# Spreading two softmax weights over 64 feature rows: GpSimd copies and transposes, or loads of DRAM rows

## The chip, the cores and the metric

One core of one Trainium2 chip. The time is the device time of one launch in microseconds; beside it stands one profiled execution, which is somewhat longer than the others. The core has TensorE (matrix products and transposes), VectorE, ScalarE, GpSimd, and a set of DMA engines. DMAs are issued from the queues of SyncE, ScalarE and GpSimd; a queue goes through its instructions in order, so an instruction that waits holds up all that is behind it on its engine.

## What is computed

Two layers of a decoder trunk on 512 tokens of width 1024. Each layer has a mixing part (windowed attention beside retention, joined by gates) and a feed-forward part. The change touches the end of the attention alone. There are three groups of six heads of 64 features: plain windows, windows with keys at every 4th token, and windows with keys at every 16th. The outputs of the groups are added with weights in proportion to their softmax denominators:

```
o   = einsum('bghnqk,bghnke->bghnqe', p / l, vb)
lse = m + log(l)
wts = softmax(stack(lses), axis=0)
y_a = sum(wts[..., None] * stack(outs), axis=0)
```

In the kernel the second and third group are computed under one softmax, in an order of tokens in which every 4th token stands together. So two "orders" are left, 0 (tokens in their own order) and 1 (token 4l + r stands at place l of part r), and each head and token has two weights.

## The kernel before

All large products are split in a high and a low half (`whi`, `wlo`) and take three matmuls each. ScalarE makes the high half by a cast (line 346), VectorE the low one by a subtraction (line 354). TensorE runs these products one after the other, and other work is threaded between them: a list of small steps (`side`), from which a step is taken each time that some matmuls have been written down. The program is written in that order. A planner then orders each engine's instructions by this order and by when it expects their inputs to be ready, so a small instruction can stand earlier on its engine than in the text.

The attention of a layer goes over three pairs of heads. For a pair, `attention_pair` makes two lists. `ops` holds, for each of four tiles of 128 tokens, the scores (line 517, with exponentials at line 535), their transposes and copies (lines 545 and 546) and the products with the values (line 558; copy to `y` at line 559), and at the end `swap`, which stores maxima and sums of order 1 to DRAM (line 573). `tail` holds what comes after: `swapped` loads them back in the order of the tokens (line 576), `weigh` computes the two weights on 128 token partitions (lines 582 to 593) and stores those of order 1 to DRAM (line 592), `weighed` loads these back in the other order (line 598). Then, for each order, `expand` copies each weight 64 times along the free dimension on GpSimd (line 605), `turn_weights` transposes the four tiles on TensorE into PSUM (line 611), so that features stand on partitions and tokens along the row as in `y`, and `combine` multiplies on VectorE and adds (lines 616 to 620).

The tail of pairs 0 and 1 is put between the steps of the next pair, at fixed places (line 959). That of pair 2 runs beside the rotary products, the value and gate products and the first retention scores (lines 965 and 1045). A tiny copy from `latest["sT"]`, the last transposed score tile (lines 582 and 597), keeps the planner from moving the step ahead of that tile.

Of the kernel before, what the change touches and what calls it, by code (L numbers as in the profile page):

```python
# [12 lines left out]
F32 = mybir.dt.float32  # L13
# [3 lines left out]
ALU = mybir.AluOpType  # L17
# [3 lines left out]
P = 128  # L21
S = 512
D = 1024
KD = D // P
NI = S // P
DEPTH = 2
HD = 64
HPG = 6
NG = 3
# [27 lines left out]
def hybrid_kernel(ctx, tc, x, x_t, w_first, rel_t, b_cols, b_rows, w_in, w_attn_proj, w_ret_proj, w_out,  # L57
# [3 lines left out]
    pe, act, dve, pool = nc.tensor, nc.scalar, nc.vector, nc.gpsimd  # L61
# [4 lines left out]
    sm = ctx.enter_context(tc.tile_pool(name="sm", bufs=4, side="right"))  # L66
    rawp = ctx.enter_context(tc.tile_pool(name="rawp", bufs=8, side="right"))
    drp = ctx.enter_context(tc.tile_pool(name="drp", bufs=1, space=DRAM))
# [34 lines left out]
    def psum(name="px"):  # L103
        return psm.tile([P, S], F32, tag="mm", name=name)
# [11 lines left out]
    def work(name):  # L116
        return wk.tile([P, S], F32, tag="w2", name=name)
# [387 lines left out]

    latest = {}

    def attention_pair(hp, qk, v, yp, bias, yaT):


        y = yp()
# [46 lines left out]
                        mm(px[cs, od * P:(od + 1) * P], vs[j][:, cs], sTs[od][:, hh, j * P:(j + 1) * P], j == j1, j == 1)  # L558
            act.copy(out=y[:, :, i], in_=px[:, :2 * P].rearrange("p (o t) -> p o t", o=2))

        fa = sm.tile([P, 2, NI, 2], F32, tag="fa", name="fa", bufs=2)
        mb = sm.tile([P, NI, 4], F32, tag="mb", name="mb", bufs=2)
        wb = sm.tile([P, NI, 2], F32, tag="wb", name="wb", bufs=2)

        exd = drp.tile([S, 4], F32, tag="exd", name="exd", bufs=2)
        exd2 = drp.tile([S, 2], F32, tag="exd2", name="exd2", bufs=2)

        def swap():

# [8 lines left out]
        def weigh():  # L578
            mn = sm.tile([P, NI, 2], F32, tag="mn", name="mn", bufs=2)
            ea = sm.tile([P, 2, NI, 2], F32, tag="ea", name="ea", bufs=2)  # L580
            wa = sm.tile([P, NI, 2], F32, tag="wa", name="wa", bufs=2)
            dve.tensor_copy(mn, latest["sT"][:, 0, P:P + 2 * NI].rearrange("p (i h) -> p i h", i=NI))
            dve.tensor_tensor(out=mn, in0=nm[:, 0], in1=mb[:, :, 0:2], op=ALU.min)
            dve.tensor_tensor(out=ea[:, 0], in0=mn, in1=nm[:, 0], op=ALU.subtract)
            dve.tensor_tensor(out=ea[:, 1], in0=mn, in1=mb[:, :, 0:2], op=ALU.subtract)
            act.activation(out=ea, in_=ea, func=AF.Exp)
            dve.tensor_tensor(out=wa, in0=ea[:, 0], in1=ls[:, 0], op=ALU.mult)
            dve.tensor_tensor(out=wb, in0=ea[:, 1], in1=mb[:, :, 2:4], op=ALU.mult)
            dve.tensor_tensor(out=wa, in0=wa, in1=wb, op=ALU.add)
            dve.reciprocal(out=wa, in_=wa)  # L590
            dve.tensor_tensor(out=wb, in0=ea[:, 1], in1=wa, op=ALU.mult)
            act.dma_start(exd2.rearrange("(i p) c -> p i c", p=P), wb)
            dve.tensor_tensor(out=fa[:, 0], in0=ea[:, 0], in1=wa, op=ALU.mult)

        def weighed():

            act.copy(out=fa[:, 1], in_=latest["sT"][:, 0, P:P + 2 * NI].rearrange("p (i h) -> p i h", i=NI))
            act.dma_start(fa[:, 1], exd2.rearrange("(l r) c -> l r c", r=4))

        wide_, weights = {}, {}  # L600

        def expand(od):

            wide_[od] = work("fe")
            pool.tensor_copy(out=wide_[od].rearrange("p (i h e) -> p i h e", i=NI, h=2),
                             in_=fa[:, od].unsqueeze(3).to_broadcast([P, NI, 2, HD]))

        def turn_weights(od):
            px = weights[od] = psum()
            for i in range(NI):  # L610
                pe.transpose(px[:, i * P:(i + 1) * P], wide_[od][:, i * P:(i + 1) * P], ident)  # L611

        def combine(od):
            yo = y[:, od].rearrange("p i t -> p (i t)")
            if od == 0:
                dve.tensor_tensor(out=yaT[:, hp], in0=yo, in1=weights[od], op=ALU.mult)
            else:
                dve.tensor_tensor(out=yo, in0=yo, in1=weights[od], op=ALU.mult)
                yr = yaT[:, hp].rearrange("p (l r) -> p r l", r=4)
                dve.tensor_tensor(out=yr, in0=yr, in1=y[:, od], op=ALU.add)  # L620

# [3 lines left out]
                places[(0, 7, 14, 20)[i] + at].append(lambda f=f, i=i: f(i))  # L625
        ops = [f for p_ in places for f in p_ or [nothing]]
        ops.append(swap)
        steps = [[lambda f=f, od=od: f(od) for f in (expand, turn_weights, combine)] for od in range(2)]
        tail = [swapped, weigh] + steps[0] + [weighed] + steps[1]
        return ops, tail  # L630

    VB = 288
# [10 lines left out]
    def layer(ly, cp):  # L643
# [12 lines left out]
        csp = yap  # L656
        cos = csp.tile([P, S], F32, name="cos")
        sin = csp.tile([P, S], F32, name="sin")

        def slot(name="op", dt=F32R):  # L660
            return opp.tile([P, 2, S], dt, tag="op", name=name)
# [62 lines left out]
        with stage("attn") as ap_, stage("attw", 4) as aw:  # L724
# [212 lines left out]
            for hp in range(HPG // 2):  # L937
                if hp:
                    for g in range(2):
                        qk_slot(hp, g)  # L940
                if hp == 2:
                    qk_put(2, 2, 1, wstat(us, 1))
                if hp:
                    qk_group((hp, 0), (hp, 1))
                if hp == 1:
                    us = qk_units(2, 2)
                    qk_slot(2, 2)
                    qk_put(2, 2, 0, wstat(us, 0))
                drain()
                ops, t_ = attention_pair(hp, [qk[hp, g] for g in range(NG)], load_v(hp), outputs_last if hp == HPG // 2 - 1 else outputs_, bias, yaT)  # L950
                if hp + 1 < HPG // 2:
                    ops.insert(17, lambda hp=hp: load_bias(hp + 1))
                if hp == 0:
                    if ly == 0:
                        for tab in (cos, sin):
                            pool.tensor_copy(out=tab[:, :1], in_=qk[0, 0][:, 0, :1])
                    pool.dma_start(cos, c_cos)
                    pool.dma_start(sin, c_sin)
                for at, f in zip((31, 30, 28, 22, 20, 18, 13, 12, 3), reversed(tail)):
                    ops.insert(at, f)  # L960
                side.extend([nothing] * (3, 3, 8)[hp] + ops)
                tail = t_
                pace(25 if hp < 2 else 32)
            n = [nothing]
            side.extend(n * 3 + tail[:1] + n * 8 + tail[1:3] + n * 2 + tail[3:4] + n * 2 + tail[4:5] + n + tail[5:6])
            pace(42)
            rotary(0)
            vg = ret_values_gates(0)
# [4 lines left out]
        with ret:  # L973
# [59 lines left out]
            for h in range(RH):  # L1033
                if h:
                    side.extend(ops)
                    pace(18)
                    rotary(h)
                    drain()
                    vg = ret_values_gates(h)
                    side.extend(turns)  # L1040
                ops = ret_scores(h)
                if h:
                    side.extend([nothing] + ops)
                else:
                    side.extend([nothing] + ops + tail[6:7] + [nothing] * 2 + tail[7:8] + [nothing] + tail[8:] + [nothing])
                pace(15 if h == 0 else 32)
                run(vg)
                drain()
                ops, turns = ret_outputs(h)
# [554 lines left out]
```

## Time and profile before

| | us |
|---|---|
| median of 3 runs | 2082.54 (2082.49 to 2083.14) |
| the profiled execution | 2089.8 |
| its span | 2088.0 |
| TensorE busy in the span | 2069.8 |
| VectorE / ScalarE / GpSimd busy | 1644.6 / 1146.5 / 252.2 |

TensorE's clock was granted at 0.998. Lines of the profile name an engine (PE is TensorE, PEld its weight load, DVE is VectorE, ACT ScalarE, POOL GpSimd), a line of the kernel, and the tiles written and read; a q behind the engine means its queue, where DMAs are issued. The DRAM tile `exd2` shows as `exd` in these rows, since trailing digits are left out, and the wide tile of weights as `fe`. Matmuls overlap, so the time that one takes from TensorE is read from the starts of neighbours, not from its duration.

### The profile page before, as it was taken

The page shows a single profiled execution, that of the slowest core. Times are in us where ns is not written, and L with a number is a line of the kernel's source. Part 1 is how long each engine was busy: PE and PEld are TensorE (multiplying, and loading weights), DVE is VectorE, ACT ScalarE, POOL GpSimd, SP SyncE. Part 2 cuts the span into 40 slices and gives each one's busy share as a digit, 9 for nine tenths or more (in the row PEclk, how much of TensorE's full clock was granted, in tenths as well). Part 3 has the DMA queues.
Part 4 walks back from the last instruction along what each step waited for, and adds up shares of the span by engine and source line. Part 5 has one row for each costly group of instructions (what it writes and reads, how often), then busy time and mean ns, then how long its engine had stood idle before and what let it go on. Part 6 is the DMA issues. An engine that isn't in the chain of part 4 may idle for free.

```text
span 2088.0 us, 33561 instructions
## 1 busy us (share of the span) xinstructions
PE 2069.8 (99%) x13090; PEld 1851.0 (89%) x13090; DVE 1644.6 (79%) x2335; ACT 1146.5 (55%) x1746; POOL 252.2 (12%) x236
## 2 busy tenths in 40 slices
PE   9999999999999999999999999999999999999998
PEld 9989888888788898999899898888888889989897
DVE  7757888786797698887777578797868877988876
ACT  6576655565654364555355766455655534655551
POOL 1001111100021101011020011111100211110101
PEclk9999999999999999999999999999999999999999
DMA  7855466766979368868258555667669882786871
GB/s 233 220 139 143 123 169 169 188 165 164 284 158 277 72 159 203 193 162 220 81 167 222 143 134 132 169 160 201 179 154 282 175 264 70 180 206 162 200 192 43
DMA packets 298991, 363.21 MB, mean 174 GB/s; under 512 B 21968, under 2 KB 209488, under 8 KB 298832
## 3 DMA queue, kind: packets, MB, share of 16 engines
q1 hardware_dynamic: 208544, 251.17, 38.0%
q0 software_dynamic: 62592, 97.01, 25.9%
q10 hardware_dynamic: 27696, 12.89, 2.2%
q8 instruction: 102, 1.67, 0.3%
q14 instruction: 57, 0.47, 0.1%
HBM read 339.45 MB, written 21.57 MB: 173 GB/s over the span
## 4 chain that ended last, share of the span: by engine, by line
PE 89%; issue 4%; DMA 3%; DVE 2%; ACT 1%; POOL 0%; ACTq 0%; SPq 0%; POOLq 0%; DVEq 0%
PE ps L96 81%; PE px L96 6%; DMA y_d<-yt 1%; PE px L545 1%; DMA raw<-in_w_in 1%; DVE wlo L354 1%; PE px L1021 1%; ACT whi L346 0%; PE px L208 0%; PE px L1234 0%; POOL ry L150 0%; DMA xc<-in_x_t 0%; ACTq L1024 0%; PE px L611 0%; DMA v_d<-sn 0%
## 5 line engine op out<-in xcount | busy, mean ns | idle before, releaser
L354 DVE TENSOR_TENSOR wlo<-raw,whi 128x1024 fp32r<-128x1024 f32 (+1 forms) x518 | 602.1, 1172 | 192.3 <-ACT whi L346 175.3
L346 ACT CAST whi<-raw 128x1024 fp32r<-128x1024 f32 (+1 forms) x518 | 516.4, 1007 | 387.7 <-PE ps L96 145.3
L96 PE MATMUL ps<-xs,whi 128*128 128x256 f32 x2176 | 399.2, 285 | 0.4 <-ACT sn L773 0.4
L96 PE MATMUL ps<-whi,xs 128*128 128x512 f32 (+1 forms) x1152 | 347.6, 372 | 0.5 <-ACT sn L487 0.5
L96 PEld LDWEIGHTS ps<-xs,whi 128*128 128x128 f32 x2176 | 339.7, 192 | 4.7 <-issue 1.7
L96 PE MATMUL ps<-xh,whi 128*128 128x256 f32 (+1 forms) x1104 | 318.7, 291 | 0.7 <-ACT xh L107 0.7
L96 PE MATMUL ps<-xl,whi 128*128 128x256 f32 (+1 forms) x1104 | 315.8, 287 | 0.1
L96 PE MATMUL ps<-xh,wlo 128*128 128x256 f32 (+1 forms) x1104 | 315.1, 286 | 0.0
L96 PE MATMUL ps<-xs,wlo 128*128 128x256 f32 x1088 | 307.9, 283 | 0.0
L96 PEld LDWEIGHTS ps<-whi,xs 128*128 128x128 f32 x1152 | 210.0, 188 | 34.9 <-ACT sn L487 0.9
L96 PEld LDWEIGHTS ps<-xh,whi 128*128 128x128 f32 x1104 | 211.1, 192 | 7.9 <-issue 1.7
L96 PEld LDWEIGHTS ps<-xl,whi 128*128 128x128 f32 x1104 | 211.7, 192 | 2.9 <-DVE xl L108 0.9
L96 PE MATMUL ps<-wlo,xs 128*128 128x512 f32 (+1 forms) x576 | 213.3, 370 | 0.8 <-DVE wlo L354 0.8
L96 PEld LDWEIGHTS ps<-xh,wlo 128*128 128x128 f32 x1104 | 211.5, 192 | 1.4
L96 PEld LDWEIGHTS ps<-xs,wlo 128*128 128x128 f32 x1088 | 208.7, 192 | 0.0
L96 PE MATMUL ps<-whi,xh 128*128 128x512 f32 (+1 forms) x512 | 194.4, 380 | 4.2 <-ACT whi L346 2.6
L96 PE MATMUL ps<-wlo,xh 128*128 128x512 f32 (+1 forms) x512 | 191.1, 374 | 0.3 <-DVE wlo L354 0.3
L96 PE MATMUL ps<-whi,xl 128*128 128x512 f32 (+1 forms) x512 | 191.1, 374 | 0.0
L337 POOL DMA_DIRECT2D raw<-in_w_in x80 | 96.2, 1209 | 717.8 <-DMA raw<-in_w_in 263.8
L370 DVE TENSOR_TENSOR raw<-raw 128x1024 f32<-128x1024 f32 (+1 forms) x148 | 171.7, 1168 | 0.8
L96 PE MATMUL ps<-whi,ht 128*128 128x512 f32 x544 | 170.2, 391 | 0.0
L107 ACT CAST whi<-raw 128x1024 fp32r<-128x1024 f32 (+1 forms) x100 | 100.0, 1016 | 84.3 <-PE ps L96 68.0
(226 smaller groups left out, 3216.3 us busy)
## 6 DMA issues: line engine op xcount, KB each, us to landing
raw<-in_w_in SPq DMA_DIRECT2D x168, 512.0 KB, 5.2
raw<-in_w_in POOLq DMA_DIRECT2D x64, 512.0 KB, 8.1
raw<-in_w_ffn_up SPq DMA_DIRECT2D x64, 512.0 KB, 4.6
raw<-in_w_ffn_down SPq DMA_DIRECT2D x52, 512.0 KB, 4.6
raw<-in_w_ffn_gate SPq DMA_DIRECT2D x44, 512.0 KB, 5.2
raw<-in_w_ffn_gate POOLq DMA_DIRECT2D x40, 512.0 KB, 6.8
raw<-in_w_in SPq DMA_DIRECT2D x48, 256.0 KB, 4.8
raw<-in_w_ret_proj SPq DMA_DIRECT2D x24, 512.0 KB, 5.8
```

The lines of the kernel that those rows point to most:

```text
L96: pe.matmul(ps, lhsT=a, rhs=b, start=start, stop=stop, skip_group_check=True)
L107: c = act.copy(out=hi, in_=src)
L337: pool.dma_start(r, self.src({"P1": "B12", "P3": "B22"}[n], u), accum_op=ALU.add)
L346: c = act.copy(out=h, in_=src)
L354: dve.tensor_tensor(out=l, in0=src, in1=h.bitcast(F32), op=ALU.subtract)
L370: dve.tensor_tensor(out=r, in0=r, in1=self.t["B22" if n == "P2" else "B21", u], op=ALU.add)
L545: pe.transpose(px[:, hh, j * P:(j + 1) * P], ss[od][:, hh, j * P:(j + 1) * P], ident)
L1021: pe.transpose(px[:, t * P:(t + 1) * P], ys[i][:, t * P:(t + 1) * P], ident)
```

## The change

The weights are no longer spread over the 64 features of a head on chip. `weigh` writes both orders' weights into one small tile and stores it to DRAM as four rows of 512 tokens (two orders, two heads), element by element. `spread` then loads for each order two of these rows, each broadcast into 64 partitions of a tile `fe` of 128 x 512. `combine` multiplies `y` by `fe`; for order 1 it reads `fe` in steps of four instead of having the weights loaded back in the other order. `weighed`, `expand` and `turn_weights` are gone, and with them the PSUM buffer of the weights. `fe` is one tile in a pool of one buffer, used by both orders and all three pairs of a layer. The tail has six steps instead of nine, at new places.

```diff
-    def attention_pair(hp, qk, v, yp, bias, yaT):
+    def attention_pair(hp, qk, v, yp, bias, yaT, fe):
...
-        fa = sm.tile([P, 2, NI, 2], F32, tag="fa", name="fa", bufs=2)
+        wt = sm.tile([P, 2, 2, NI], F32, tag="fa", name="wt", bufs=2)
...
-        exd2 = drp.tile([S, 2], F32, tag="exd2", name="exd2", bufs=2)
+        exd2 = drp.tile([4, S], F32, tag="exd2", name="exd2", bufs=2)
...
             dve.reciprocal(out=wa, in_=wa)
-            dve.tensor_tensor(out=wb, in0=ea[:, 1], in1=wa, op=ALU.mult)
-            act.dma_start(exd2.rearrange("(i p) c -> p i c", p=P), wb)
-            dve.tensor_tensor(out=fa[:, 0], in0=ea[:, 0], in1=wa, op=ALU.mult)
-
-        def weighed():
-
-            act.copy(out=fa[:, 1], in_=latest["sT"][:, 0, P:P + 2 * NI].rearrange("p (i h) -> p i h", i=NI))
-            act.dma_start(fa[:, 1], exd2.rearrange("(l r) c -> l r c", r=4))
-
-        wide_, weights = {}, {}
-
-        def expand(od):
-
-            wide_[od] = work("fe")
-            pool.tensor_copy(out=wide_[od].rearrange("p (i h e) -> p i h e", i=NI, h=2),
-                             in_=fa[:, od].unsqueeze(3).to_broadcast([P, NI, 2, HD]))
-
-        def turn_weights(od):
-            px = weights[od] = psum()
-            for i in range(NI):
-                pe.transpose(px[:, i * P:(i + 1) * P], wide_[od][:, i * P:(i + 1) * P], ident)
+            for od in range(2):
+                dve.tensor_tensor(out=wt[:, od].rearrange("p h i -> p i h"), in0=ea[:, od], in1=wa, op=ALU.mult)
+            act.dma_start(exd2.rearrange("q (i p) -> p q i", p=P), wt.rearrange("p o h i -> p (o h) i"))
+
+        def spread(od):
+
+            act.copy(out=fe[:, :2 * NI], in_=latest["sT"][:, 0, P:P + 2 * NI])
+            for h in range(2):
+                act.dma_start(fe[h * HD:(h + 1) * HD], exd2[2 * od + h].partition_broadcast(HD))
 
         def combine(od):
-            yo = y[:, od].rearrange("p i t -> p (i t)")
             if od == 0:
-                dve.tensor_tensor(out=yaT[:, hp], in0=yo, in1=weights[od], op=ALU.mult)
+                dve.tensor_tensor(out=yaT[:, hp], in0=y[:, od].rearrange("p i t -> p (i t)"), in1=fe, op=ALU.mult)
             else:
-                dve.tensor_tensor(out=yo, in0=yo, in1=weights[od], op=ALU.mult)
+                dve.tensor_tensor(out=y[:, od], in0=y[:, od], in1=fe.rearrange("p (l r) -> p r l", r=4), op=ALU.mult)
...
-        steps = [[lambda f=f, od=od: f(od) for f in (expand, turn_weights, combine)] for od in range(2)]
-        tail = [swapped, weigh] + steps[0] + [weighed] + steps[1]
+        tail = [swapped, weigh] + [lambda f=f, od=od: f(od) for od in range(2) for f in (spread, combine)]
...
+        fe = yap.tile([P, S], F32, name="fe")
...
-                for at, f in zip((31, 30, 28, 22, 20, 18, 13, 12, 3), reversed(tail)):
+                for at, f in zip((31, 24, 23, 16, 11, 3), reversed(tail)):
...
-            side.extend(n * 3 + tail[:1] + n * 8 + tail[1:3] + n * 2 + tail[3:4] + n * 2 + tail[4:5] + n + tail[5:6])
+            side.extend(n * 3 + tail[:1] + n * 8 + tail[1:2] + n * 4 + tail[2:3] + n * 6 + tail[3:5])
...
-                    side.extend([nothing] + ops + tail[6:7] + [nothing] * 2 + tail[7:8] + [nothing] + tail[8:] + [nothing])
+                    side.extend([nothing] + ops + tail[5:] + [nothing])
```

More of the change, by code (lines that the diff above doesn't have):

```diff
@@ L949, in layer @@
                 drain()
-                ops, t_ = attention_pair(hp, [qk[hp, g] for g in range(NG)], load_v(hp), outputs_last if hp == HPG // 2 - 1 else outputs_, bias, yaT)
+                ops, t_ = attention_pair(hp, [qk[hp, g] for g in range(NG)], load_v(hp), outputs_last if hp == HPG // 2 - 1 else outputs_, bias, yaT, fe)
                 if hp + 1 < HPG // 2:
```

## The prediction

> **What bounds the kernel now.** I read the page first: span, busy times, chain of waits. Then the two stretches in which the weights are applied (one per layer), by the busy time of each engine; then the lines of the change, group by group; then the timeline of TensorE and of ScalarE around one of them.
>
> ```profile
> span 2088.0 us, 33561 instructions
> PE 2069.8 (99%) x13090; PEld 1851.0 (89%) x13090; DVE 1644.6 (79%) x2335; ACT 1146.5 (55%) x1746; POOL 252.2 (12%) x236
> PE 89%; issue 4%; DMA 3%; DVE 2%; ACT 1%; POOL 0%; ACTq 0%; SPq 0%; POOLq 0%; DVEq 0%
> ```
> ```profile
> 120.00:295.00 175.00, 175.00 (x1240) 154.21 (x1239) 133.77 (x263) 110.90 (x227) 21.34 (x21) 1.00 0.54 130
> 1162.00:1337.00 175.00, 175.00 (x1243) 154.43 (x1242) 132.98 (x262) 110.96 (x228) 20.92 (x22) 1.00 0.54 131
> ```
>
> The chain of waits is TensorE for 89% of the span. In the second fence (window, length, then PE, PEld, DVE, ACT and POOL busy, granted clock, DMA share) TensorE is busy for all 175 us of both stretches, while VectorE is busy for 133.77 / 175 = 76% and ScalarE for 63%. So in the stages that the change touches TensorE sets the time. An instruction taken off it shortens the program by what it occupies, as long as nothing that feeds it comes later than now. A page that is busy throughout does not prove that each matmul runs at its pace, so the pace is read from starts, below.
>
> **What is removed: the transposes.** The lines of the change, in the view by groups (busy us, mean ns of one, idle time before them):
>
> ```profile
> L611 PE MATMUL px<-ident,fe 128*128 128x128 f32 x48 | 7.2, 272 | 0.0
> L605 POOL COPY fe<-fa 128x512 f32<-128x512 f32 x12 | 12.0, 1001 | 117.8 <-DVE fa L593 61.3 <-PE px L96 28.4 <-DVE nm L532 23.0
> L620 DVE TENSOR_TENSOR yaT<-yaT,y 128x512 f32<-128x512 f32 x6 | 6.6, 1093 | 0.1
> ```
>
> 48 transposes in 12 groups of four. Their 272 ns overlap, so the price is read from starts (start, duration) in the timeline of TensorE, once alone among projections and once behind other transposes:
>
> ```profile
> 156.65 0.40 PE L96 MATMUL ps<-xs,whi 128*128 128x256 f32 x2
> 156.89 0.28 PE L96 MATMUL ps<-xs,wlo 128*128 128x256 f32 x1
> ...
> 157.37 0.60 PE L611 MATMUL px<-ident,fe 128*128 128x128 f32 x4
> 157.72 0.48 PE L96 MATMUL ps<-xs,whi 128*128 128x256 f32 x2
> 158.04 0.28 PE L96 MATMUL ps<-xs,wlo 128*128 128x256 f32 x1
> ```
> ```profile
> 169.40 1.04 PE L545 MATMUL px<-ident,s 128*128 128x128 f32 x8
> 170.28 0.60 PE L611 MATMUL px<-ident,fe 128*128 128x128 f32 x4
> 170.81 0.43 PE L96 MATMUL px<-s,v 128*64 128x128 f32 x2
> ```
>
> Alone, the four hold TensorE from 157.37 to 157.72 = 0.35 us, and the two matmuls behind them take 158.04 - 157.72 = 0.32 instead of 156.89 - 156.65 = 0.24, so 0.43 us. Behind others, 170.81 - 170.28 = 0.53 us, of which about 0.1 is a change of kind that the eight L545 then pay themselves, so again 0.43. Twelve groups: 12 x 0.43 = 5.2 us (5.8 if the 0.53 went whole in half of them). The two PSUM buffers that each pair took for the weights come free too; nothing on TensorE waited for them.
>
> The GpSimd copies (12.0 us busy) go, and the waits of GpSimd's queue ahead of them, 117.8 us in all. Behind them on that queue stand the accumulating weight loads. They will be issued earlier, but in these stretches TensorE does not stand for a weight, so I count 0.
>
> **What is added.** Landing times (KB each, median us from issue to landing) of the DMAs of this place and of the nearest others, and the spread of the store of line 592:
>
> ```profile
> cos<-const_cos POOLq DMA_DIRECT2D x2, 256.0 KB, 5.2
> exd<-pk ACTq DMA_DIRECT2D x6, 8.0 KB, 1.4
> mb<-exd ACTq DMA_DIRECT2D x6, 8.0 KB, 1.8
> exd<-wb ACTq DMA_DIRECT2D x6, 4.0 KB, 4.6
> ```
> ```profile
> L592 ACTq DMA_DIRECT2D exd<-wb x6: 372/377/378, 151.0 to 1270.7; - x6
> DMA to landing us min/median/max: 4.1/4.6/7.2
> ```
>
> (1) The store of the weights. Before, 128 x 4 runs of 8 bytes; after, 128 x 16 single elements of 4 bytes, 2048 runs. A store of 128 runs (pk) lands in 1.4 us, one of 512 runs (wb) in 4.6, a load of 512 runs in 1.8: it is many small runs written to DRAM that cost. Bounds: if the extra is one delay for any such store, 4.1 (the least of line 592); if it grows with the runs, 1.4 + 4 x (4.6 - 1.4) = 14.2 us. No row decides; between them, (4.1 + 14.2) / 2 = 9.2 us, and both ends go into the range. The Trainium skill speaks against this store (DMA: Bandwidth & Descriptors, Rules for kernel authors): a last dimension that is not contiguous becomes one descriptor per element, and should be made contiguous. By the same page of the Trainium skill (section Bandwidth), about 10.5 ns a packet, 2048 of them would be an estimated 21.5 us, and 512 an estimated 5.4, where the trace has 4.6. By its section Anatomy of one DMA most of a nearly constant 2 us is the wait for the write's receipt, and the sum would stay as it is.
>
> (2) Who stands behind it. ScalarE issues the loads of the weights, and it can't pass them until the store has landed; its evictions, exponentials and casts are queued behind. Its timeline from the store on (L592), in the pair where the least lies between:
>
> ```profile
> 151.01 0.37 ACTq L592 DMA_DIRECT2D exd<-wb  x1
> ...
> 156.46 0.35 ACT L559 COPY y<-px 128x256 f32<-128x256 f32 x1
> 157.09 1.05 ACT L346 CAST whi<-raw 128x1024 fp32r<-128x1024 f32 x1 [0.27 <-PE ps L96]
> 158.04 0.58 ACT L773 COPY sn<-ps 128x512 f32<-128x512 f32 x1
> 160.39 1.05 ACT L346 CAST whi<-raw 128x1024 fp32r<-128x1024 f32 x1 [1.76 <-PE ps L96]
> 161.34 0.58 ACT L773 COPY sn<-ps 128x512 f32<-128x512 f32 x1
> 161.82 1.08 ACT L546 COPY s<-px 128x512 f32<-128x512 f32 x2
> ```
> ```profile
> 166.12 1.10 PE L96 MATMUL px<-s,v 128*64 128x128 f32 x16
> ```
>
> Five steps after the weights comes the first spread, just ahead of line 559: 156.46 - 151.01 = 5.4 us after the issue. So with 9.2 us ScalarE stands for 3.8. Its own idle time before the copies of line 546 is 0.27 + 1.76 = 2.0 us, and these copies end at 162.9, while TensorE takes them up at 166.12: 3.2 more. TensorE feels a landing later than 5.4 + 2.0 + 3.2 = 10.6 us. At 9.2 the cost is 0, and that is the cover: past 10.6 each us of landing is a us of TensorE, in this place and its like in the other layer. In the second pair ScalarE comes to line 559 later:
>
> ```profile
> 191.73 0.38 ACTq L592 DMA_DIRECT2D exd<-wb  x1
> ...
> 202.56 0.35 ACT L559 COPY y<-px 128x256 f32<-128x256 f32 x1
> ```
>
> 10.8 us lie between, so nothing stands there at 9.2, and at 14.2 the 3.4 us that it would stand are under the 3.2 + 2.0 of cover. In the last pair, which runs beside rotary and values:
>
> ```profile
> 227.95 0.38 ACTq L592 DMA_DIRECT2D exd<-wb  x1
> ...
> 232.60 0.34 ACTq L598 DMA_DIRECT2D fa<-exd  x1
> 233.06 1.05 ACT L346 CAST whi<-raw 128x1024 fp32r<-128x1024 f32 x1 [1.07 <-PE ps L96]
> ```
>
> Here ScalarE already stands for the store today: line 598 goes 4.65 us after line 592, and TensorE lost nothing. The cast behind it is due at 233.06, 5.1 us after the store, and serves a product that begins about one product later: 24 matmuls of 512 columns, at twice the 0.12 us that one of 256 took above, 5.8 us, less the cast's 1.05 and a subtraction of about 1.1 (line 620's length): cover 5.1 + 3.6 = 8.7 at the least. At 9.2 that would be 0.5 us in each layer; since five steps of the side list lie between and let other work go first, I count 0, and 2 x 0.5 = 1.0 as the other end.
>
> (3) The loads: per order one short copy and two loads of 64 rows, in place of one copy and one load for the pair. That is 3 more issues of up to 0.38 and one copy that is smaller than line 559's 0.35, at most 1.5 us of ScalarE per pair, 9 us over six pairs, in stretches where it is 63% busy: 0. Two loads of 128 KB are 256 KB, 5.2 us by the tables' row (cos); the combination is seven steps behind, and if five steps were 5.4 us above, seven are some 7.6: covered. If the cover is gone, VectorE stands and the subtractions behind it come late by the same amount.
>
> (4) One tile for both orders: the second spread's copy must wait on ScalarE for the first combination on VectorE, right ahead of it, at most 1.1 us by the row of line 620; behind it on ScalarE stand the last exponentials. It was put at the combination's own place, so I count some 1 us of ScalarE's idle time a pair, 0 on TensorE. (5) The second multiplication now reads its weights with a step of four: line 620 is the row for such a step, so at most 1.1 us each and 6.6 in all on VectorE, under the 24% that it is idle: 0.
>
> **Sum.** -5.2 us of TensorE, everything else 0 with bounds 0 to 1.0 at the landing I take. The profiled execution took 2089.8 us for a span of 2088.0, 7.3 above the median of the runs, 2082.5; the share is the same to a hundredth, so I take the 5.2 from the median: 2082.5 - 5.2 = 2077.3 us.
>
> **Rivals.** *ScalarE stands for the store (slower).* One mechanism: the 2048 runs land late, ScalarE blocks at the first spread, the transposed scores and casts come late. Loss = 2 x (L - 10.6) + 2 x (L - 8.7) for a landing L. It eats the whole 5.2 from L = (5.2 + 38.6) / 4 = 11 us on, and is slower by over 0.2% from 12.0. At 14.2: 2 x 3.6 + 2 x 5.5 = 18.2, so 2095.5. For it: 128 to 512 runs went from 1.4 to 4.6. Against: a load of 512 runs takes 1.8, ScalarE already stood for a store without a loss, and the planner orders ScalarE's work by when it thinks the store lands, so other work may go first. By the rate of the Trainium skill named above (DMA: Bandwidth & Descriptors, Bandwidth), 21.5 us, the same formula gives an estimate of 2077.3 + 2 x 10.9 + 2 x 12.8 = 2124.7.
> *The gain is waited away (no change, 2082.5).* TensorE is let go 5.2 us earlier and then stands for VectorE or ScalarE, which do no less than before, or a landing of 10 to 12 gives part or all of it back, 2079 to 2086. For: VectorE's 76%. Against: 175 of 175 us without a stand.
> *More than the sum.* The 0.53 counts whole, and the new order of the work takes away one of the few waits of TensorE that the view of waits shows (us, times, longest):
>
> ```profile
> PE ps L96 <- DVE sn L494: 1.5, 3, 0.8
> ```
>
> 2082.5 - 5.8 - 1.5 = 2075.2. *It doesn't do what it says* has no room: the transposes are gone from the code.
>
> **Chances.** Forecast 0.47, more than the sum 0.05, gain waited away or mostly given back 0.26, slower 0.22. What a measurement of this kernel tells from no change is about 0.2%, 4.2 us; the forecast is just past that. Faster 0.52, same 0.26, slower 0.22. The range reaches from 2075.2 into the slower case, to a landing of 12.6: 2077.3 + 2 x 2.0 + 2 x 3.9 = 2089. The forecast's own range, with both ends of its small terms, is 2075 to 2079.
>
> **What would show it.** Right: no line 611 and no GpSimd copy, TensorE's count lower by 48, the starts of neighbouring projections closed up, no idle TensorE between 120 and 295. Wrong: in the landing of the store of the weights more than 10.6 us, ScalarE idle ahead of the first spread's loads by more than 5 us, and TensorE idle with ScalarE's copies of scores or a cast as its releaser; or VectorE idle ahead of a combination with a load as releaser.

## The result, and the profile after

The changed kernel takes 2152.61 us (median of 6 runs, 2150.81 to 2155.8) against 2084.47 for the kernel before beside it (6 runs, 2082.49 to 2089.52). The ratio is 1.0316, with a 95% interval of 1.0303 to 1.0329: about 68 us slower. The forecast was 2077.3 with a range of 2075.2 to 2089.0, so both the sign and the range were wrong. All that follows reads one profiled execution of it, 2155.8 us for a span of 2154.0, beside the one of before.

The page of the changed kernel: span, busy times, the granted clock in 40 slices, and the chain of waits.

```profile
span 2154.0 us, 33451 instructions
PE 2084.2 (97%) x13042; PEld 1860.2 (86%) x13042; DVE 1644.1 (76%) x2335; ACT 1146.3 (53%) x1752; POOL 241.7 (11%) x224
...
PEclk9998899999999999999999988999999999999999
...
PE 79%; DMA 8%; issue 5%; DVE 4%; ACT 3%; POOL 0%; ACTq 0%; SPq 0%; POOLq 0%; DVEq 0%
```

TensorE did 48 instructions less (13042 against 13090) and was nevertheless busy for 14.4 us more (2084.2 against 2069.8). The span less the busy time gives its idle time: 69.8 us against 18.2 before, 51.6 more. 51.6 + 14.4 = 66.0 us, the difference of the spans. So there are two questions: what TensorE waited for, and why less work kept it busy longer. The clock row already shows where: slices 4 and 5 and 24 and 25 are the two stretches in which the weights are applied.

The same two stretches as in the prediction, by engine (window, length, PE, PEld, DVE, ACT, POOL busy, granted clock, DMA share, GB/s):

```profile
120.00:295.00 175.00, 147.11 (x998) 127.54 (x997) 101.21 (x204) 91.65 (x202) 10.91 (x11) 0.90 0.51 110
1162.00:1337.00 175.00, 157.86 (x1163) 139.43 (x1162) 102.84 (x220) 98.20 (x229) 10.33 (x10) 0.93 0.57 128
```

Before, TensorE was busy for all 175 us of both, at a clock of 1.00. VectorE and ScalarE were also busy for less time in these stretches than before (101.21 against 133.77, 91.65 against 110.90): everyone is waiting for someone.

Who waits, in three views: the landing of the new DMAs; the waits that VectorE and ScalarE owe to them (releaser's target: us in total, times), first for the store of line 593, then for the tile `fe`; and TensorE's own waits (us in total, times, longest).

```profile
fe<-exd ACTq DMA_DIRECT2D x24, 128.0 KB, 5.9
...
exd<-wt ACTq DMA_DIRECT2D x6, 8.0 KB, 12.4
```
```profile
L593 ACTq DMA_DIRECT2D exd<-wt x6: 366/366/377, 149.5 to 1323.3; - x6
...
ACT s L535: 36.1, 4
ACT whi L346: 22.3, 2
...
DMA to landing us min/median/max: 11.5/12.4/13.0
```
```profile
DVE yaT L603: 56.5, 6
```
```profile
PE ps L96 <- ACT sn L487: 21.9, 2, 11.4
PE px L545 <- ACT s L535: 13.7, 4, 5.3
PE ps L96 <- ACT sn L760: 10.4, 3, 5.3
PE ps L96 <- DVE sn L768: 5.2, 2, 2.7
```

The store lands after 12.4 us (4.6 before). ScalarE stands 58.4 us behind it, six times; VectorE stands 56.5 us, six times, at the first combination (line 603), for loads that could not start before the store had landed. These four rows of TensorE's waits add up to 51.2 us. All but one wait of 0.4 us, ahead of the second layer's stores, are for evictions or exponentials that stood behind one of those two stands, or (line 768) behind the second combination, whose loads the stands had made late.

One pair in the order of time, on ScalarE, VectorE and TensorE (start, us, engine, line; in brackets the idle time before it and its releaser):

```profile
149.48 0.37 ACTq L593 DMA_DIRECT2D exd<-wt  x1
...
154.33 0.20 ACT L597 COPY fe<-s 128x8 f32<-128x8 f32 x1
161.09 1.15 ACTq L599 DMA_DIRECT2D fe<-exd  x2
162.28 0.51 ACT L535 ACTIVATE s<-s,nm 128x256 f32<-128x256 f32 x1 [7.75 <-issue]
...
164.26 0.56 ACT L760 COPY sn<-ps 128x512 f32<-128x512 f32 x1
```
```profile
167.91 0.69 DVE L603 TENSOR_TENSOR yaT<-y,fe 128x512 f32<-128x512 f32 x1 [11.98 <-DMA fe<-exd]
```
```profile
159.87 0.28 PE L96 MATMUL ps<-xs,wlo 128*128 128x256 f32 x1
164.88 0.80 PE L96 MATMUL ps<-xs,whi 128*128 128x256 f32 x2 [4.73 <-ACT sn L760]
```

ScalarE issues the store at 149.48 and comes to the first spread at 154.33. The loads leave at 161.09, 11.6 us after the store, and only then the exponentials and the eviction of line 760 (the row of line 773 before) go on. TensorE has run out of free PSUM at 159.87 + 0.28 = 160.15 and stands until 164.88.

The last pair of the layer, on ScalarE, VectorE and TensorE:

```profile
248.09 0.37 ACTq L593 DMA_DIRECT2D exd<-wt  x1
...
261.12 1.16 ACTq L599 DMA_DIRECT2D fe<-exd  x2
262.39 1.99 ACT L346 CAST whi<-raw 128x1024 fp32r<-128x1024 f32 x2 [11.41 <-issue]
269.21 0.20 ACT L597 COPY fe<-s 128x8 f32<-128x8 f32 x1 [4.83 <-DVE yaT L603]
269.55 1.11 ACTq L599 DMA_DIRECT2D fe<-exd  x2
270.71 0.58 ACT L487 COPY sn<-ps 128x512 f32<-128x512 f32 x1 [1.30 <-issue]
```
```profile
268.48 0.69 DVE L603 TENSOR_TENSOR yaT<-y,fe 128x512 f32<-128x512 f32 x1 [13.79 <-DMA fe<-exd]
```
```profile
271.34 0.79 PE L96 MATMUL ps<-whi,xs 128*128 128x512 f32 x1 [11.36 <-ACT sn L487]
```

This is a chain of four links. The loads wait for the store (13.0 us), the first combination waits for the loads (to 268.48), the second spread's copy on ScalarE waits for that combination because both orders share one tile (4.83 us), and the eviction of line 487, for which TensorE waits, stands behind the second spread. TensorE loses 11.4 us at once.

What the waits do to the work that follows them, in the same columns as the stretches above:

```profile
162.60:169.40 6.80, 4.52 (x20) 4.21 (x22) 1.49 (x2) 6.23 (x16) 0.00 (x0) 0.50 0.45 137
...
179.60:186.50 6.90, 6.19 (x32) 5.97 (x34) 3.10 (x4) 2.97 (x4) 0.00 (x0) 0.51 0.05 4
...
265.00:275.20 10.20, 3.86 (x10) 3.28 (x11) 3.56 (x4) 3.17 (x5) 1.28 (x1) 0.50 0.62 125
```

Around these stands TensorE's granted clock falls to half (0.50 and 0.51 in the last column but two) for 6.8 or 10.2 us, and what it does in that time takes nearly twice as long (the matmuls that start at 165.69 take 0.43 us to the next start, the same ones at 159.63 took 0.24): this is where the additional busy time comes from. There are four such stretches in the first layer, at 162.6, 179.6, 217.2 and 265.0, and four in the second. TensorE is busy for 42.5 us in the eight; if half of that is the slowing, it is 21 us, enough for the 14.4. The kernel before had one such place, elsewhere: behind a stand of 2.6 us for a cast of line 346, its clock was 0.51 from 525.8 to 529.2. The Trainium skill (TensorE: Matmul & The Clock Gate, Part 1) says that the clock is halved after an idle window of about 3.4 us and restored after a busy one. The trace agrees with the window, since the half-clock stretches are two and three times 3.4 us. A full 3.4 us of standing was not needed, for the stretch at 179.6 lies around a stand of 2.5 us; a stand of 2.6 us at 283.9 left the clock as it was.

### The profile page after: what moved, and what is told of

Same layout as the page of the kernel before. It is cut to its first block, busy times and chain, and to the rows that moved or that the text cites. A ratio compares the mean times of both kernels' runs of the same rounds, so it can differ in the third digit from the quotient of the medians.

```text
span 2154.0 us, 33451 instructions
## 1 busy us (share of the span) xinstructions
PE 2084.2 (97%) x13042; PEld 1860.2 (86%) x13042; DVE 1644.1 (76%) x2335; ACT 1146.3 (53%) x1752; POOL 241.7 (11%) x224
## 4 chain that ended last, share of the span: by engine, by line
PE 79%; DMA 8%; issue 5%; DVE 4%; ACT 3%; POOL 0%; ACTq 0%; SPq 0%; POOLq 0%; DVEq 0%
PE ps L96 73%; PE px L96 4%; DMA exd<-wt 3%; DMA fe<-exd 2%; DVE wlo L354 2%; DMA raw<-in_w_in 1%; ACT s L535 1%; DMA y_d<-yt 1%; ACT whi L346 1%; PE px L1008 1%; PE px L545 0%; PE px L208 0%; DVE raw L370 0%; PE px L1221 0%; POOL ry L150 0%
```

## The experiments

The theory that these rows suggested was: one cause, the store. It lands late, ScalarE's queue stands behind it, and all else follows. The rivals were the single tile for both orders, the loads being on ScalarE's queue at all, and the places of the combinations on VectorE.

**A store of fewer runs.** The changed kernel with this one edit:

```diff
-act.dma_start(exd2.rearrange("q (i p) -> p q i", p=P), wt.rearrange("p o h i -> p (o h) i"))
+act.dma_start(exd2.rearrange("q (a b) -> (q a) b", b=4 * NI), wt.rearrange("p o h i -> p (o h i)"))
```

> The changed kernel with one edit: the store of the weights writes each partition's 16 values as one run of 64 bytes (128 runs) instead of 2048 runs of 4. The weights so stand at other places in DRAM than the loads take them for, and are multiplied with the wrong tokens; the number of instructions, bytes and loads is that of the changed kernel. Theory 1 (the store of 2048 runs sets the loss: ScalarE stands for its landing, 11.5 to 13.0 us, and VectorE behind it): the store lands in 1.4 to 2 us, ScalarE no longer stands, the loss of 68 us goes, and if the 5.2 us of the removed transposes are real the time is 2077 to 2080. Theory 2 (the loads, the one tile and the places of the steps cost on their own): the store lands early but VectorE still stands at the combinations; 2100 to 2140. Theory 3 (the time of the transposes is waited away): 2082 to 2086.

Measured: 2105.0 us, ratio 1.0082 (1.0062 to 1.0102); 47.6 us of the 68 are gone. What is left shows in its landing times and in the same pair, on VectorE and TensorE:

```profile
exd<-wt ACTq DMA_DIRECT2D x6, 8.0 KB, 3.2
```
```profile
169.44 1.11 DVE L605 TENSOR_TENSOR y<-y,fe 128x512 f32<-128x512 f32 x1 [3.31 <-DMA fe<-exd]
...
173.96 0.68 DVE L768 TENSOR_TENSOR sn<-sn,ps 128x512 f32<-128x512 f32 x1
```
```profile
174.70 0.39 PE L96 MATMUL ps<-xh,whi 128*128 128x256 f32 x1 [3.70 <-DVE sn L768]
```

The store lands in 3.2 us (1.4 to 5.0) and ScalarE no longer stands. But VectorE still waits 3.3 us for the second spread's loads, and behind the combination, the addition and two instructions for other weights stands the eviction of line 768, for which TensorE waits 3.7 us. So with the short store most of the loss goes, and not all of it.

**A tile for each order**, with the store of 2048 runs as in the change:

```diff
+        fes = {0: fe}
...
+            if od:
+                fes[od] = work("fe")
+            fe = fes[od]
...
```

> The changed kernel with one edit: the weights of the second order go to a tile of their own, so that the second spread needn't wait for the first combination. Theory 1 (the store): the wait of ScalarE for the first combination (9.6 us in two places) goes, the store's stays: some 2 to 10 us less, 2142 to 2151. Rival (the one tile chains spread and combination and so makes the loss): 2082 to 2110.

Measured: 2135.88 us, ratio 1.0237 (1.0214 to 1.0259), 16.7 less than the change. The shared tile is a real part of the price, through the third link of the last pair's chain: TensorE's stand there falls from 11.4 to 6.4 us, though a subtraction of line 354 brings another 2.6 right behind it. VectorE's stand at the first combination stays (43.9 us, five times).

**The loads on GpSimd's queue**, so that ScalarE does not wait for the store:

```diff
-                act.dma_start(fe[h * HD:(h + 1) * HD], exd2[2 * od + h].partition_broadcast(HD))
+                pool.dma_start(fe[h * HD:(h + 1) * HD], exd2[2 * od + h].partition_broadcast(HD))
```

> The changed kernel with one edit: the four loads of a pair are issued from GpSimd's queue instead of ScalarE's; the store stays as it is. Theory 1a (ScalarE, blocked at the loads, is what TensorE stands for): ScalarE runs on, and most of the loss goes: 2085 to 2105. Theory 1b (VectorE, standing 56.5 us at the first combinations for the late weights, stops TensorE as well): 2125 to 2150 even with ScalarE free.

Measured: 2151.64 us, ratio 1.0312 (1.0288 to 1.0336), as slow as the change. Who waited for `fe` in this kernel:

```profile
DVE yaT L603: 66.9, 6
ACT fe L597: 34.4, 4
```
```profile
PE px L545 <- DVE nm L532: 21.6, 4, 9.4
```

ScalarE no longer waits for the store, and VectorE pays instead: it stands 66.9 us at the first combination. TensorE's largest wait is now for VectorE's pass over the scores (line 532), which stands behind that combination. That refuted the theory that ScalarE's wait for the store is the mechanism: the delay runs through two in-order queues. In the second pair of a layer VectorE's queue alone stops TensorE (9.4 us in the second layer). In the first and the third ScalarE stands as well, now 34.4 us for VectorE at the second spread's copy, so what VectorE's queue alone would cost in the whole kernel, with a tile for each order, no run here shows.

**The store by itself, all to one tile**: the kernel before with six such stores of zeros, all to one spare DRAM tile, and nothing that reads them.

```diff
...
+                act.dma_start(spare.rearrange("q (i p) -> p q i", p=P), small.rearrange("p (q i) -> p q i", q=4))
```

> The kernel before, plus six stores of 2048 runs of 4 bytes that nobody reads or waits for, three in each layer's feed-forward part where weights are loaded all the time; they write zeros to a spare place. It measures what such a store does to other transfers. If the store only lands late and takes nothing from others (its packets take 1 us of the DMA engines): landing 11 to 13 us and the time of before within 2 us. If it holds the DMA engines while it drains (the trace of the changed kernel moves some 30 KB per us behind it, where 200 are usual): each store keeps weights back by 7 to 9 us; eight weight buffers of 512 KB hold some 20 us of products ahead, so 0 to 10 us in all, with TensorE or ScalarE waiting for raw.

Measured: 2130.92 us, ratio 1.0214 (1.0198 to 1.0231). It does not answer the question asked. Nothing tied the stores to their place, so the planner put all six at the start of the program, and since they write one tile, each waited on ScalarE's queue for the one before, from 2 to 77 us. What it does show: a landing of 11 to 14 us where nothing else of the change is present, and a price of 45 us when ScalarE's queue is held by it.

**The store by itself, unread**: each with a tile of its own, tied to its place in the feed-forward part by a copied value.

```diff
+                small = sm.tile([P, 16], F32, tag="small", name="small", bufs=2)
+                act.copy(out=small, in_=v[:, 0, :16])
+                spare = drp.tile([4, S], F32, name=f"spare{ly}{f}")
+                act.dma_start(spare.rearrange("q (i p) -> p q i", p=P), small.rearrange("p (q i) -> p q i", q=4))
```

> The kernel before, plus six stores of 2048 runs of 4 bytes to a spare place of their own each, three in each layer's feed-forward part, tied to that place by a copy of a value computed there; nobody reads them or waits for them. (The fourth run was meant to be this, but its stores had no tie: the planner put all six at the start, and each waited on ScalarE's queue for the one before.) If such a store lands late but takes nothing from the weights: 2084 to 2088. If it holds the DMA engines for the 8 to 10 us in which it drains, weights land that much later: with all cover gone 6 x 9 = 54 us, with the eight weight buffers as cover 0 to 20 us, and TensorE or ScalarE waiting for raw behind each.

Measured: 2086.26 us, ratio 1.0004 (0.9991 to 1.0017), with this landing:

```profile
spare<-small ACTq DMA_DIRECT2D x6, 8.0 KB, 11.3
```

A store as late as in the change costs nothing here, where no one waits for it. So here the price is the wait, not the traffic. In the change the traffic suffers all the same: while the store is under way, the core's DMA engines move little else. A window of the changed kernel up to the store's landing, then the same window of the kernel with the short store (last three columns: clock, DMA share, GB/s):

```profile
152.00:161.00 9.00, 8.15 (x76) 7.34 (x74) 3.59 (x10) 2.50 (x6) 0.00 (x0) 1.00 0.31 19
```
```profile
152.00:161.00 9.00, 9.00 (x85) 8.40 (x84) 4.23 (x12) 7.20 (x18) 0.00 (x0) 1.00 0.58 169
```

19 GB/s against 169. These two windows don't separate the store from transfers that were not yet issued because their buffers came free late. The unread stores do: in the 10 us behind each of the six, the core moved 16 to 43 GB/s, and 246 to 321 in the 10 us after that, where the kernel before moved 46 to 156 and 201 to 215 in the same windows. So such a store holds other transfers back while it lands, though nothing waits for it; they are made up for right behind it, and in the feed-forward part the time does not feel it. What this costs in the stage of the change no run shows by itself.

**What makes the store late**: the kernel before with three unread transfers of other forms in the same place, two of each.

```diff
+            if f == 4:
+                act.dma_start(spare.rearrange("q (p c) -> p q c", p=P), small.rearrange("p (q c) -> p q c", q=4))
+            elif f == 8:
+                act.dma_start(spread_out[:, :, 0], small)
+            else:
+                act.dma_start(spare[0].rearrange("(i p) -> p i", p=P), small[:, :4])
```

> The kernel before with three unread small transfers in the feed-forward part of each layer, from ScalarE's queue and each with a buffer of its own: 512 runs of 16 bytes to DRAM, 512 runs of 4 bytes to DRAM, and 2048 runs of 4 bytes to a tile on chip. It asks what makes the change's store land late (12.4 us at 2048 runs of 4 bytes to DRAM, 4.6 at 512 runs of 8 bytes). If the number of runs sets it, the two of 512 runs land in 4 to 5 us each, and that of 2048 runs to the chip lands in 11 to 13. If it is small writes to DRAM, the last lands in 2 to 4 us. If it is the size of a run, the 4-byte runs to DRAM land much later than the 16-byte ones at the same count. The time stays within 0.3% of before, since nothing waits for them.

```profile
spare<-small ACTq DMA_DIRECT2D x2, 8.0 KB, 2.5
spread_out<-small ACTq DMA_DIRECT2D x2, 8.0 KB, 4.3
spare<-small ACTq DMA_DIRECT2D x2, 2.0 KB, 9.0
```

512 runs of 16 bytes land in 2.5 us, 2048 runs of 4 bytes to a tile on chip in 4.3, and only 512 runs of 4 bytes to DRAM in 9.0. So the number of runs is not what counts most: at 4 bytes, 512 runs (9.0) and 2048 runs (11.3) differ by a quarter, and at 512 runs the landing goes 2.5, 4.6 (line 592 before, 8 bytes), 9.0 as the run goes 16, 8, 4 bytes. In all of these, neighbouring partitions write neighbouring bytes of DRAM, so the shorter the run, the more of them fall into one short stretch of it. That such writes go one after the other would fit these numbers, but no run here varies it alone. The Trainium skill (DMA: Bandwidth & Descriptors, Specifications) says that transfers under 512 bytes are done by reading, changing and writing back; by that alone 512 runs of 16 bytes should be as late as 512 of 4 bytes, and they are not (2.5 against 9.0). The one execution took 2087.47 us, 0.14% over the 2084.6 of the kernel before beside it; each form was seen twice in it.

**Late combinations, with the change's store.** The changed kernel with a tile for each order, the loads on GpSimd's queue, both spreads in neighbouring steps, and the two combinations at the end of the next pair's list; on VectorE they are ordered behind the last eviction that stands ahead of them in the text.

```diff
-                dve.tensor_tensor(out=yaT[:, hp], in0=y[:, od].rearrange("p i t -> p (i t)"), in1=fe, op=ALU.mult)
+                late(dve.tensor_tensor(out=yaT[:, hp], in0=y[:, od].rearrange("p i t -> p (i t)"), in1=fes[0], op=ALU.mult))
...
-                for at, f in zip((31, 24, 23, 16, 11, 3), reversed(tail)):
+                for at, f in zip((len(ops), 30, 17, 16, 11, 3), reversed(tail)):
```

> The changed kernel, its store of 2048 runs and its output as they are, with its waits moved out of the way: the loads from GpSimd's queue (as in the third run), a tile for each order, both spreads at the old place of the first, the combinations 7 to 20 steps later behind an eviction. If the waits of ScalarE and VectorE are all of the loss: 2078 to 2090. If the store itself holds the weight loads and small exchanges of the same stage: 2095 to 2130 in spite of that.

Measured: 2103.79 us, ratio 1.0087 (1.0063 to 1.0111). The long store is still there, and most of its price is gone: what it held up is now asked for later. The time lies in the range of the expectation's second case, but waits are left too: VectorE stands 26.1 us for the loads, four times. In the second pair of each layer the loads are still late, on VectorE and then on ScalarE (here in the first layer):

```profile
213.31 0.69 DVE L617 TENSOR_TENSOR yaT<-y,fe 128x512 f32<-128x512 f32 x1 [10.48 <-DMA fe<-exd]
```
```profile
214.71 0.62 ACT L111 CAST rot<-sn 128x512 fp32r<-128x512 f32 x1 [10.98 <-DVE sn L672]
```

So the short store alone (-47.6 us) and this later asking alone (-48.8: two tiles, GpSimd's queue and late combinations together) each take away some 48 us, and their sum would be more than the whole: much of the time needs both a late store and a combination that asks too early.

**Both together**: the short store of the first experiment, two tiles and the late combinations, the loads on ScalarE's queue.

> The kernel of the first run (store of 128 runs, so the weights are misplaced and the output is not the reference's), and in addition the loads are taken off VectorE's way: both spreads follow each other at the old place of the first, the second order has a tile of its own, and the two combinations come 7 to 20 steps later, each ordered behind the last eviction of a product on VectorE that is written before it. It asks where the rest, 2105 against 2086, comes from. Theory A (the loads land in 5 us, later than planned, VectorE stands 27 us for them in ten places with evictions behind it, and TensorE feels that): no wait for them is left and the 5.2 us of the transposes show: 2078 to 2083 where before is 2084 to 2086. Theory B (something else in the new tail, or the transposes' time isn't to be had): 2086 to 2105.

Measured: 2081.09 us, ratio 0.9977 (0.9961 to 0.9993). The whole loss is gone, and VectorE no longer waits for `fe`. 2105.0 - 2081.09 = 24 us (23 when each is taken against the kernel before beside it) is what the early combinations and the shared tile still cost with a short store.

**Long runs in the change's own layout.** The 16 weights of a token are turned once by TensorE and stored as 16 runs of 512 bytes:

```diff
-            act.dma_start(exd2.rearrange("q (i p) -> p q i", p=P), wt.rearrange("p o h i -> p (o h) i"))
+            px = psum()
+            pe.transpose(px[:16, :P], wt.rearrange("p o h i -> p (o h i)"), ident)
+            wtT = sm.tile([16, P], F32, tag="wtT", name="wtT", bufs=1)
+            act.copy(out=wtT, in_=px[:16, :P])
+            act.dma_start(exd2.rearrange("q (i p) -> (q i) p", p=P), wtT)
```

First the turned store alone, all else as in the change:

> The changed kernel with its store alone turned: one TensorE transpose of the 16 weights a token, a copy by ScalarE, and a store of 16 runs of 512 bytes. Nothing else is moved, the tile is one for both orders and the places of the tail are those of the change. If the price is made of two parts, the store (about 47 us) and the loads that catch VectorE ahead of an eviction (about 24 us), this kernel still pays the second: about 2100 to 2108 us, with the store landing under 5 us and VectorE waiting for the loads at the combinations. If the short store of misplaced weights was slower than before only for a reason of its own, and a turned store is enough, it comes out at 2080 to 2086 us.

Measured: 2100.98 us, ratio 1.0077 (1.006 to 1.0094), the second price alone: the store lands in 2.7 us, and VectorE stands 26.1 us for the loads, eight times. With two tiles and the late combinations too, the loads on ScalarE's queue:

> A correct version without the short runs: one transpose per pair turns the 128 x 16 weights to 16 x 128, ScalarE copies them from PSUM, and the store is 16 runs of 512 bytes; loads, two tiles and late combinations as in the fifth run. One group of one transpose in place of two of four leaves 5.2 - 6 x 0.2 = some 4 us of gain (0.43 was the price of four with the change of kind, one is 0.1 and the change). If the store lands in 1.5 to 3.5 us and the loads are covered: 2079 to 2084 where before is 2084 to 2086. If the loads still catch VectorE: 2086 to 2105.

Measured: 2081.9 us, ratio 0.9989 (0.9974 to 1.0004). Its store, then its first stretch:

```profile
L605 ACTq DMA_DIRECT2D exd<-wtT x6: 324/324/334, 151.8 to 1269.0; - x6
...
DMA to landing us min/median/max: 1.4/1.4/4.3
```
```profile
120.00:295.00 175.00, 174.84 (x1228) 153.26 (x1227) 135.30 (x264) 112.90 (x235) 15.64 (x15) 1.00 0.55 140
```

TensorE is busy nearly throughout again, at full clock, and nothing waits for `fe`. The same kernel once more:

> The kernel with the turned store, a tile for each order and the late combinations once more, since its first interval just reached 1.000. It has six small transposes and six copies more than nothing, so it should be a little behind the kernel without transposes: ratio 0.998 to 0.999. If it is no better than before, 1.000.

Measured: 2084.0 us, ratio 0.9991 (0.9979 to 1.0002). Twice a thousandth below the kernel before, and both times with an interval that still holds 1.000: this form of the idea costs nothing, and whether it gains 2 us is not settled.

**What the transposes are worth.** The kernel before without them, and nothing in their place:

```diff
-            px = weights[od] = psum()
-            for i in range(NI):
-                pe.transpose(px[:, i * P:(i + 1) * P], wide_[od][:, i * P:(i + 1) * P], ident)
+            weights[od] = wide_[od]
```

> The kernel before with the 48 transposes of the weights taken out and nothing put in their place: the combinations read the tile that GpSimd wrote, so the weights are left unturned (this part of the computation is left out). It prices the first term of the sum by itself. If the 5.2 us of TensorE are real and nothing else comes late, 5 us faster than the kernel before of the same call, ratio 0.9975, near the kernel with misplaced weights (0.9977). If TensorE only waits the gain away, ratio 1.000, and the 0.9977 came from another part.

Measured: 2082.99 against 2085.94 us, ratio 0.9988 (0.9977 to 1.0000): 2.5 us, between 0 and 4.8. TensorE's busy time fell by 4.4 us (2069.8 to 2065.4):

```profile
PE 2065.4 (99%) x13042; PEld 1845.7 (88%) x13042; DVE 1643.9 (79%) x2335; ACT 1145.5 (55%) x1746; POOL 251.6 (12%) x236
```

## Why the prediction was wrong

**The transposes, 5.2 us: nearly right in TensorE's work, less in the time.** 4.4 us of busy time go, and 2.5 us of the run (0 to 4.8). The whole prize is then about a thousandth, under the 0.2% that the prediction named as the bound of what can be told from no change. With no loss at all, "the same" would have been the better forecast.

**(1) The store: the size was inside the bounds, the reason was not.** Taken 9.2, measured 12.4, bounds 4.1 and 14.2. The upper bound let the landing grow with the number of runs; the three forms show that the landing goes with the length of the run in DRAM, or with how many runs share a stretch of it, far more than with their number: 512 runs of 4 bytes already land in 9.0. Why that is so stays open. The rule of the Trainium skill (DMA: Bandwidth & Descriptors, Rules for kernel authors) to make the last dimension contiguous pointed the right way: the turned store follows it and lands in 1.4 to 2.7. The estimate of 21.5 us from that page's section Bandwidth, whose figure was taken on loads that GpSimd issues, was too high for 12.4 measured.

**(2) The cover: this, with the cover of (3), is the step that failed.** The prediction let TensorE feel a landing later than 10.6 us, and nothing at all in the second pair. Two of its readings were wrong.
First, the slack of 3.2 us was read from the copies of the transposed scores (line 546). The first thing that TensorE missed was another one, the eviction of a projection (line 760), which frees PSUM. In the first pair TensorE ran out at 160.15, 10.7 us after the store's issue; but between the landing and its return at 164.88 lie 3.8 us of work queued on ScalarE (two issues, four exponentials, the eviction: from 161.09). The cover was 10.7 - 3.8 = 6.9 us, and 11.6 - 6.9 = 4.7 is the wait that the profile shows. Even the 9.2 us that the prediction took would have cost 2.3 here.
Second, where ScalarE comes to the spread was taken from where it came to line 559 in the kernel before: 10.8 us after the store in the second pair. In the changed kernel it is 3.3 us, and ScalarE stands for 9.9:

```profile
205.13 0.37 ACTq L593 DMA_DIRECT2D exd<-wt  x1
...
208.38 0.20 ACT L597 COPY fe<-s 128x8 f32<-128x8 f32 x1
217.22 1.19 ACTq L599 DMA_DIRECT2D fe<-exd  x2
218.46 0.51 ACT L535 ACTIVATE s<-s,nm 128x256 f32<-128x256 f32 x1 [9.88 <-issue]
```

The copy of the spread reads only the transposed scores, which are there early, and the planner puts a small instruction where it can go; the loads behind it then wait in the queue.

**(3) The loads: said to be covered by 7.6 us.** They land in 5.9 us, near the 5.2 taken. But the cover was counted from a spread in time, and the loads left 11.6 to 13.0 us after the store's issue. The run with the loads on GpSimd's queue shows that this cover weighs as much as (2): with ScalarE out of the store's way the loss was the same. VectorE's stand of 56.5 us is what the prediction had named as the price "if the cover is gone", without giving it a chance or a size. Even with a short store the cover isn't there: 24 us remain until the combinations are moved.

**(4) One tile: counted as 1 us of ScalarE a pair and 0 on TensorE.** A tile for each order gives 16.7 us back. The wait is short only if the first combination is on time; when it is late, the second spread carries VectorE's lateness into ScalarE's evictions.

**(5) The second multiplication: right.** It reads its weights in steps of four and takes 1.07 to 1.12 us, as line 620 did (1.09).

**The rival "ScalarE stands for the store" had the sign and the first link**, and a price that was too small by a factor of nearly seven: by its formula a landing of 12.4 gives 2 x 1.8 + 2 x 3.7 = 11 us on top of 2077.3, and the kernel took 75 us more than that. It missed the cover's real size, VectorE as a second path (the loads on GpSimd's queue leave ScalarE free of the store's wait and cost as much), and the clock. The clock's part: TensorE's busy time rose by 14.4 us while the transposes took 4.4 away, so some 19 us of the 66 are work drawn out by the half clock. No term of the prediction had this; the rows that it quoted show the clock at 1.00.

## What to carry to other kernels

A small DMA whose result is soon needed is priced by two numbers, its landing and the first instruction behind its wait that another engine is about to need; take the second from evictions that free PSUM as well as from data, and add the work queued between the wait and that instruction. A step that is added must not be given the place of a step that it resembles: an instruction with early inputs moves up, and its wait moves up with it. Where weights have to go through DRAM, turn them on chip first so that the runs are long, and let the consumer ask late.

## What the runs showed of the hardware

- The landing of a small store to DRAM went with the length of its runs: 16 bytes 2.5 us, 8 bytes 4.6, 4 bytes 9.0, each at 512 runs; 2048 runs of 4 bytes 11.3 to 12.5 to DRAM and 4.3 to a tile on chip; 128 runs of 64 bytes 1.4 to 3.2 and 16 runs of 512 bytes 1.4 to 2.7, by the kernel.
- While such a store of 2048 runs landed, the core's other transfers fell to 16 to 43 GB/s, with nothing waiting for it, and rose to 246 to 321 right behind it.
- TensorE's granted clock halved for 6.8 or 10.2 us around eight of the nine stands of over 2.4 us in the changed kernel. A wait of a few us thus costs more than its length: 51.6 us more of standing came with work that took some 19 us longer.
